# Gathering expert rows in a mixture-of-experts stage: one float32 copy and one pair of experts at a time, in place of two rounded copies and two pairs

## Chip, cores and metric

The kernel runs on one core of a Trainium2 chip, as one program. The metric is the device time of one execution in microseconds. It is compared with the same program with the change applied; the inputs, the outputs and the arithmetic asked for are the same.

## What is computed

The program is a whole block of a model: a first layer with two mixers and a mixture of experts, then two layers of another kind. The change touches the mixture of experts of the first layer alone. There are 256 tokens of width 1024, 32 experts in 4 groups, and each token goes to its two best experts of its best group. Cut to that part, the reference is:

```python
def hier_moe(h, w_rg, b_rg, w_re, b_re, w_eg, w_eu, w_ed):
    t = h.reshape(-1, d)                       # 256 x 1024, rmsnorm(x, norm2_g)
    lg = (t @ w_rg) + b_rg                     # 4 groups
    _, g_idx = lax.top_k(lg, 1)
    le = einsum('nd,dge->nge', t, w_re) + b_re # 8 experts in each group
    ...
    gates = sum(one_hot(eid) * (pg_sel * pw))  # 256 x 32, two entries in a row
    for e in range(32):
        hid = silu(t @ w_eg[e]) * (t @ w_eu[e])     # 1024 -> 512
        out = out + gates[:, e:e + 1] * (hid @ w_ed[e])  # 512 -> 1024
    return out
```

All of it is float32, and the three weights of an expert are 2 MB each, 192 MB for the 32 experts.

## The kernel before

**Tokens and places.** The tokens lie on the 128 partitions in two halves, `t` = 0 and 1. Each expert has 64 places for the tokens that come to it. `route` (from line 826 on) finds for each token its two experts and, by a product with a triangular matrix, its place in each; the result is `R`. `select` compares `R` with the numbers 1 to 64 and so makes a matrix of zeros and ones, tokens by places. A product of the normed tokens with that matrix, over both halves, gathers an expert's tokens; it comes out turned, width on the partitions and places on the columns, as `XT`.

**The pieces of h2.** `moe_rows` squares and turns each new half row of x (ScalarE and TensorE), and with the second half calls `rstd`, `route`, `select` and `moe_split`. The last makes two tiles of the rounded type float32r: `h2h`, the normed x rounded (ScalarE, L818), and `h2l`, what the rounding left (VectorE, L819). In `gather` (`add`, L960) both are multiplied with the selection of four experts (256 columns), each for both halves of the tokens: 8 pieces of the width x 2 x 2 = 32 products of 128 x 128 by 256. `turned` (L974, L976) scales by the norm's weight and copies the result out of PSUM, half of it on VectorE and half on ScalarE.

**The loop** takes 16 pairs of experts, i = 0 to 15. `front` multiplies the gathered tokens with the pair's `w_eg` and then `w_eu` (L1071); the two experts stand on the two halves of the array's columns, so each product has 64 columns of stationary operand. `hidden` computes silu(a) times b. `down` multiplies with `w_ed` one iteration later (L1098), and `scatter` brings the result back to the tokens one more iteration later (L1045, L1046, and the adds L1049). `middle` turns the hidden layer and the selection (L1017, L1025) and picks the gates (L1085). The order of TensorE's work is written out by hand: the calls named in the small tables given to `front` and `down` are put between their products. In every odd iteration but the last, four banks of the gather for the next two pairs are put among the products, two in the second `front` and two in `down`.

**Loads.** Each weight of an expert comes in two halves of 1 MB, on SyncE's queue, in the order of `expert_order`. They go round 18 slots: 8 of `wq`, 4 of `wp`, 6 of `wr` (`nwr`, L1947). `experts` takes four halves for one `front` or `down`, and four more are issued behind it (`expert_halves`). In the last round, from load 162 on, `wp` is left to the next layer's loads.

**The start of the stage.** For each half `t` of the tokens: add to x (L728), squares and transposes (L800, L803, L804), eight products with the router's weights (L834), a chain of small operations on VectorE up to the assignment `Asg` (L838 to L859), the places (L863 to L865), the selection (L824). For t = 1, `keep_warm` (L133) puts two products with zeros behind the router's. The first gather has its own order: t = 0 early, t = 1 when it can. `route_rest` counts the tokens of the fullest expert, and every engine branches on that count before the loop begins (L1108, L1109).

Of the kernel before, what the change touches and what calls it, by code (L numbers as in the profile page):

```python
# [19 lines left out]
P = 128  # L20
# [72 lines left out]
class K:  # L93
# [687 lines left out]
    def moe_open(self, es, e0):  # L781
# [14 lines left out]
    def moe_rows(self, x, t, n):  # L796
# [3 lines left out]
        nc.scalar.activation(self.h2l[:, t, cs], x[:, t, cs], AF.Square, accum_out=self.ss2[:, t, n:n + 1])  # L800
# [3 lines left out]
        nc.scalar.copy(self.hT32[:, 4 * n:4 * n + 4, t * P:(t + 1) * P], ps)  # L804
        if n == 1:
            r = self.rstd(self.ss2[:, t, 0:1], 1, D, 0, self.m1, self.ss2[:, t, 1:2])
            self.route(t, r)
            self.select(self.sel0, t, self.rt["R"], 0)
            self.moe_split(x, t, r)

    def moe_split(self, x, t, r):

        nc = self.nc
        for n in range(2):
            part = lambda z: z[:, t, n * 512:(n + 1) * 512].rearrange("p (k d) -> p d k", k=4)
# [11 lines left out]
    def route(self, t, r):  # L827
# [10 lines left out]
        v.scalar_tensor_tensor(T["L"], ps[:, 0:36], r[:, 0:1], self.br, op0=ALU.mult, op1=ALU.add)  # L838
# [99 lines left out]
    def moe(self, x, es, e0):  # L938
        nc, tc, A = self.nc, self.tc, self.A
        wg, wu, wd = A["w_eg"][0], A["w_eu"][0], A["w_ed"][0]  # L940
        p, h2h, h2l = self.m1, self.h2h, self.h2l
# [8 lines left out]
        def select(R_, e0, ne, pool, name):  # L950
            sel = pool.tile([P, NT, ne, 64], F32R, name=name, bufs=1)
# [3 lines left out]

        def gather(sel, n, XT=None):


            def add(ps, k, j, t, hp, start, stop, **kw):
                return nc.tensor.matmul(ps[:, j, :n], hp[:, t, (k + j) * P:(k + j + 1) * P],  # L960
                                        sel[:, t].rearrange("p e s -> p (e s)"), start=start, stop=stop, **kw)

            def bank(k):

                ps = self.mx.tile([P, 2, 256], F32, name="mx")
                for j in range(2):
                    for i, (hp, t) in enumerate(((h2h, 0), (h2h, 1), (h2l, 0), (h2l, 1))):
                        add(ps, k, j, t, hp, i == 0, i == 3)
                return ps

            def turned(k, ps, XT):
                if k % 4:
                    for j in range(2):
                        nc.scalar.activation(XT[:, k + j, :n], ps[:, j, :n], AF.Copy, scale=self.g2[:, k + j:k + j + 1])  # L974
                else:
                    nc.vector.tensor_tensor(XT[:, k:k + 2, :n], ps[:, :, :n],  # L976
                                            self.g2[:, k:k + 2].unsqueeze(2).to_broadcast([P, 2, n]), op=ALU.mult)

            if XT is None:
                return bank, turned  # L980

            banks = self.accT() + self.accT()
            with tc.high_priority(offset=3000):
                for hp in (h2h, h2l):
                    for ps, k in zip(banks, range(0, 8, 2)):
                        for j in range(2):
                            ins = add(ps, k, j, 0, hp, hp is h2h and j == 0, False, skip_group_check=True)
                            if hp is h2h and j == 0:
                                head = ins
                            elif hp is h2h:  # L990
                                tc.add_manual_dep(ins.ins, head.ins.name, mybir.DependencyInfo(
                                    mybir.DependencyClass.NoSync, mybir.DependencyReason.DATA))
            for ps, k in zip(banks, range(0, 8, 2)):
                for j in range(2):
                    add(ps, k, j, 1, h2h, False, False, skip_group_check=True)
            for ps, k in zip(banks, range(0, 8, 2)):
                for j in range(2):
                    add(ps, k, j, 1, h2l, False, True, skip_group_check=True)
                turned(k, ps, XT)

# [20 lines left out]
        def places(selw, rows, f=""):  # L1021

            pt = self.tp.tile([P, 4, P], F32, name="tp")
            for t in range(NT):
                nc.tensor.transpose(pt[:rows, t, :], selw[:, t].bitcast(F32), self.ident)  # L1025
# [25 lines left out]
        def scatter_last(sT, py, gs, po):  # L1051

            X2 = q.tile([P, 4, 512], F32, name="x2", tag="XT", bufs=1)
            for n in range(2):
                yh, yl = parts(py, n, P, gs)
                for t in range(NT):
                    nc.tensor.matmul(po[t][n], sT[:, t], yh, start=False, stop=False)
                for t in range(NT):
                    self.mm_last = nc.tensor.matmul(po[t][n], sT[:, t], yl, start=False, stop=True)
                    x2 = X2[:, 2 * n + t]  # L1060
# [4 lines left out]
        def front(ps, XT, i, between={}):  # L1065

            o = 2 * (i % 2)
            ww = self.experts()
            for k in range(8):
                for z in range(2):  # L1070
                    nc.tensor.matmul(ps[64 * z:64 * z + 64], XT[:, k, 64 * (o + z):64 * (o + z + 1)], ww[z][k],  # L1071
# [984 lines left out]
```

## Time and profile before

| | |
|---|---|
| median of 3 runs | 1799.76 us (1799.75 to 1799.99) |
| the profiled execution | 1796.94 us |
| its span | 1795.2 us |
| TensorE busy | 1738.4 us (97%) |
| VectorE, ScalarE, GpSimd busy | 976.9, 741.5, 112.2 us |
| moved by DMA | 414.51 MB, 231 GB/s on average |
| expert loads (three weights) | 192 of 1024 KB |

Times are microseconds from the start of the span. The stage in question runs from about 150 to about 633 us, the loop of the experts from 178.5 us on. In the page's 40 slices (45 us each), DMA moves 419 or 420 GB/s in all slices from the sixth to the thirteenth, and TensorE is at 9 tenths or more in nearly all. A matmul's recorded duration has its way through the array in it, and neighbours overlap; what a stream of them costs is the distance between their starts.

### The profile page before, as it was taken

To read this page: it belongs to the slowest core of one execution; us is meant where nothing else is said; L and a number is where in the kernel's file an instruction comes from. 1 tells how busy PE (TensorE), PEld (TensorE's weight loads), DVE (VectorE), ACT (ScalarE), POOL (GpSimd) and SP (SyncE) were. 2 spreads that over 40 slices of the span, in tenths; PEclk is the share of its full clock that TensorE was granted. 3 is DMA by queue.
4 is the path that set the end of the run, shared out by engine and by line. 5 is a ranking of instruction groups with operands and counts; after the bars stand their busy time and mean duration, and the time that the engine had idled before them with its cause. 6 is when DMAs were issued, how large, how long until landed. Compare 5 with 4: busy or idle time off the path is not lost. (4 is left out here: it accounts for less than half of the span.)

```text
span 1795.2 us, 27162 instructions
## 1 busy us (share of the span) xinstructions
PE 1738.4 (97%) x10927; PEld 1327.7 (74%) x10927; DVE 976.9 (54%) x1864; ACT 741.5 (41%) x1260; POOL 112.2 (6%) x157
## 2 busy tenths in 40 slices
PE   7999999999999989999999999999999999999998
PEld 6877433343334368799979999987879988999997
DVE  7676132222222177665666665557766467676555
ACT  3454111111011145565555454444556465455443
POOL 4110000000000040000012000003000001100000
PEclk8989999999999999999999999999999999999999
DMA  8447999999999964247545755554325644455552
GB/s 262 153 185 308 379 420 419 419 420 419 419 420 419 407 196 142 65 126 224 165 144 156 234 188 188 188 189 154 111 80 170 195 143 152 145 184 188 188 188 83
DMA packets 153465, 414.51 MB, mean 231 GB/s; under 512 B 13347, under 2 KB 42868, under 8 KB 128632
## 3 DMA queue, kind: packets, MB, share of 16 engines
q1 hardware_dynamic: 152408, 410.49, 63.8%
q0 software_dynamic: 784, 2.18, 0.3%
q8 instruction: 87, 1.43, 0.3%
q14 instruction: 42, 0.34, 0.1%
q10 hardware_dynamic: 144, 0.07, 0.0%
HBM read 411.63 MB, written 2.12 MB: 230 GB/s over the span
## 5 line engine op out<-in xcount | busy, mean ns | idle before, releaser
L170 DVE TENSOR_TENSOR wlo<-raw,whi 128x1024 fp32r<-128x1024 f32 (+4 forms) x372 | 440.3, 1184 | 305.9 <-ACT whi L169 305.2
L169 ACT CAST whi<-raw 128x1024 fp32r<-128x1024 f32 (+4 forms) x384 | 385.6, 1005 | 385.5 <-PE acc L231 156.6
L231 PE MATMUL acc<-xTl,whi 128*128 128x256 f32 x992 | 286.1, 290 | 1.2 <-DVE xTl L385 1.2
L231 PE MATMUL acc<-xTh,whi 128*128 128x256 f32 x992 | 286.0, 290 | 0.0
L231 PE MATMUL acc<-xTh,wlo 128*128 128x256 f32 x992 | 279.7, 289 | 0.0
L1071 PE MATMUL acc<-raw,XT 128*64 128x512 f32 x1024 | 237.7, 602 | 2.5 <-DMA raw<-in_w_eg 1.3
L231 PEld LDWEIGHTS acc<-xTl,whi 128*128 128x128 f32 x992 | 192.9, 195 | 6.8 <-issue 5.0
L231 PEld LDWEIGHTS acc<-xTh,whi 128*128 128x128 f32 x992 | 192.8, 195 | 6.5 <-issue 5.9
L231 PEld LDWEIGHTS acc<-xTh,wlo 128*128 128x128 f32 x992 | 189.2, 194 | 5.3 <-issue 4.9
L1071 PEld LDWEIGHTS acc<-raw,XT 128*64 128x64 f32 x1024 | 69.9, 137 | 127.5 <-issue 120.9
L178 PE MATMUL acc<-wlo,xTh 128*128 128x512 f32 (+4 forms) x368 | 129.7, 353 | 0.0
L177 PE MATMUL acc<-whi,xTh 128*128 128x512 f32 (+4 forms) x368 | 129.4, 352 | 0.0
L179 PE MATMUL acc<-whi,xTl 128*128 128x512 f32 (+4 forms) x368 | 128.5, 349 | 0.0
L1098 PE MATMUL acc<-raw,hidT 128*64 128x512 f32 x512 | 118.3, 596 | 1.4 <-DMA raw<-in_w_ed 1.4
L177 PE MATMUL acc<-whi,ffh 128*128 128x512 f32 x256 | 100.9, 394 | 0.0
L178 PE MATMUL acc<-wlo,ffh 128*128 128x512 f32 x256 | 100.7, 393 | 0.0
L179 PE MATMUL acc<-whi,ffl 128*128 128x512 f32 x256 | 100.7, 393 | 0.0
L1098 PEld LDWEIGHTS acc<-raw,hidT 128*64 128x64 f32 x512 | 36.5, 137 | 68.7 <-issue 61.2
L1036 DVE SCALAR_TENSOR_TENSOR yl<-acc,gs,yh 128x512 fp32r<-128x512 f32 x32 | 24.0, 751 | 103.8 <-ACT yh L1035 103.8
L1035 ACT ACTIVATE yh<-acc,gs 128x512 fp32r<-128x512 f32 x32 | 22.0, 687 | 136.5 <-PE acc L1098 136.5
L178 PEld LDWEIGHTS acc<-wlo,xTh 128*128 128x128 f32 x368 | 69.6, 189 | 8.3 <-issue 2.1
L177 PEld LDWEIGHTS acc<-whi,xTh 128*128 128x128 f32 x368 | 69.7, 189 | 7.5 <-issue 1.2
(687 smaller groups left out, 3128.6 us busy)
## 6 DMA issues: line engine op xcount, KB each, us to landing
raw<-in_w_in SPq DMA_DIRECT2D x70, 1024.0 KB, 5.2
raw<-in_w_eg SPq DMA_DIRECT2D x64, 1024.0 KB, 19.9
raw<-in_w_eu SPq DMA_DIRECT2D x64, 1024.0 KB, 19.9
raw<-in_w_ed SPq DMA_DIRECT2D x64, 1024.0 KB, 19.9
raw<-in_w_ff SPq DMA_DIRECT2D x64, 1024.0 KB, 5.1
raw<-in_w_out SPq DMA_DIRECT2D x12, 1024.0 KB
raw<-in_w_branch SPq DMA_DIRECT2D x12, 1024.0 KB, 5.8
raw<-in_w_in SPq DMA_DIRECT2D x8, 792.0 KB
```

What stands on the lines that cost most here:

```text
L169: nc.scalar.copy(hi[:, :nk, :n], src)
L170: ins = (nc.gpsimd if pool else nc.vector).tensor_sub(lo[:, :nk, :n], src, hi[:, :nk, :n])
L177: mm(ps, ahi, bhi, start=start, stop=False)
L178: mm(ps, ahi, blo, start=False, stop=False)
L179: self.mm_ins = mm(ps, alo, bhi, start=False, stop=stop)
L231: ins = mm(ps[c // 2][:, c % 2, :], w[:, j, c * P:(c + 1) * P], x[:, kx + k + j, :], start=first and c % 2 == 0, stop=k + j == nk - 1 and ...
L1035: nc.scalar.activation(yh[:rows], py[n][:rows], AF.Copy, scale=gs)
L1036: nc.vector.scalar_tensor_tensor(yl[:rows], py[n][:rows], gs, yh[:rows].bitcast(F32), op0=ALU.mult, op1=ALU.subtract)
L1071: nc.tensor.matmul(ps[64 * z:64 * z + 64], XT[:, k, 64 * (o + z):64 * (o + z + 1)], ww[z][k], start=k == 0, stop=k == 7)
L1098: nc.tensor.matmul(py[n][64 * z:64 * z + 64], hT[:, k, 64 * z:64 * z + 64], ww[z][k][:, n * 512:(n + 1) * 512], start=k == 0, stop=k == 3)
```

## The change

`h2h` and `h2l` become one tile `h2` in float32, and the second product with `h2l` goes, and with it L819. The gather is made for one pair of experts (128 columns) in place of two pairs (256 columns), in every iteration from 0 to 14, as plain float32 products: 8 pieces x 2 halves = 16 products of 128 x 128 by 128, in two banks of four pieces. The first bank is put behind the sixth piece of the second `front`, the second one behind the second step of `down` (for i = 0, behind the second `front`). VectorE alone copies them out. The selections take three buffers of two experts, `XT` two buffers of 128 columns, and the last scatter's scratch is cut to fit those. `nwr` goes from 6 to 7, so the loads go round 19 slots; the last round, without `wp`, then begins at load 152 and has 15. The router's eight products are written as two times four, each with its half of the row, and `keep_warm` behind them goes.

```diff
-        self.h2h = p.tile([P, NT, D], F32R, name="h2h")
-        self.h2l = p.tile([P, NT, D], F32R, name="h2l")
+        self.h2 = p.tile([P, NT, D], F32, name="h2")
-        self.sel0 = p.tile([P, NT, 4, 64], F32R, name="sel", bufs=1)
+        self.sel0 = p.tile([P, NT, 2, 64], F32, name="sel", bufs=3)
...
         nc.scalar.copy(self.hT32[:, 4 * n:4 * n + 4, t * P:(t + 1) * P], ps)
+        if n == 0:
+            self.logits = self.mx.tile([P, 512], F32, name="mx")
+        for k in range(4 * n, 4 * n + 4):
+            nc.tensor.matmul(self.logits[:, 0:36], self.hT32[:, k, t * P:(t + 1) * P], self.wr[:, k, :],
+                             start=k == 0, stop=k == 7)
...
-            h, lo = part(self.h2h), part(self.h2l)
             nc.scalar.activation(h, xs, AF.Copy, scale=r[:, 0:1])
-            nc.vector.scalar_tensor_tensor(lo, xs, r[:, 0:1], h.bitcast(F32), op0=ALU.mult, op1=ALU.subtract)
...
-        ps = self.mx.tile([P, 512], F32, name="mx")
-        for k in range(8):
-            ins = nc.tensor.matmul(ps[:, 0:36], self.hT32[:, k, t * P:(t + 1) * P], self.wr[:, k, :],
-                                   start=k == 0, stop=k == 7)
-        if t:
-            self.keep_warm(self.tp, "tp", 2, ins)
...
+            def add(ps, k, t, start, **kw):
+                return nc.tensor.matmul(ps[:, k % 4, :n], h2[:, t, k * P:(k + 1) * P],
+                                        sel[:, t].rearrange("p e s -> p (e s)"), start=start, stop=t == 1, **kw)
             def bank(k):
-                ps = self.mx.tile([P, 2, 256], F32, name="mx")
-                for j in range(2):
-                    for i, (hp, t) in enumerate(((h2h, 0), (h2h, 1), (h2l, 0), (h2l, 1))):
-                        add(ps, k, j, t, hp, i == 0, i == 3)
+                ps = self.mx.tile([P, 4, P], F32, name="mx")
+                for j in range(k, k + 4):
+                    for t in range(NT):
+                        add(ps, j, t, t == 0)
                 return ps
             def turned(k, ps, XT):
-                if k % 4:
-                    for j in range(2):
-                        nc.scalar.activation(XT[:, k + j, :n], ps[:, j, :n], AF.Copy, scale=self.g2[:, k + j:k + j + 1])
-                else:
-                    nc.vector.tensor_tensor(XT[:, k:k + 2, :n], ps[:, :, :n], ...
+                nc.vector.tensor_tensor(XT[:, k:k + 4, :n], ps[:, :, :n], ...
...
-            group, banks = i % 2 and i < 15, {}
-            if group:
-                sels[i // 2 + 1] = sel = select(R, 2 * i + 2, 4, p if i % 4 == 3 else q, "sel")
-                bank, turned = gather(sel, 256)
-            front(pu, XT, i, {0: (lambda: spread(1)) if i > 1 else lambda: None,
-                              5: lambda: take(0), 6: lambda: take(2)})
+            if i < 15:
+                sels[i + 1] = sel = select(R, 2 * i + 2, 2, p, name="sel", bufs=3)
+                bank, turned = gather(sel)
+                XT1, banks = q.tile([P, 8, P], F32, name="XT"), {}
+                take = lambda k: banks.update({k: bank(k)})
+                put = lambda k: turned(k, banks[k], XT1)
+            front(pu, XT, i, {0: (lambda: spread(1)) if i > 1 else lambda: None, 5: lambda: take(0)})
+            put(0)
             hid[i] = hidden(pg, pu, P)
...
             if i:
-                ys[i - 1] = down(mid[i - 1][0], {1: lambda: put(4), 3: lambda: put(6)})
+                ys[i - 1] = down(mid[i - 1][0], {1: lambda: take(4)})
+            else:
+                take(4)
+            put(4)
...
-        k.cnt, k.nwr, k.ready, k.order = 0, 6, deque(), k.expert_order()
+        k.cnt, k.nwr, k.ready, k.order = 0, 7, deque(), k.expert_order()
```

## Rows read from the trace of the kernel before

**Rows 1.** Busy time by stretch: us; PE, PEld, DVE, ACT, POOL; clock; DMA share; GB/s

```profile
178.50:500.00 321.50, 315.82 (x1512) 127.43 (x1513) 80.37 (x149) 44.86 (x85) 0.00 (x0) 1.00 1.00 413
500.00:620.00 120.00, 114.44 (x529) 47.25 (x528) 28.18 (x48) 15.97 (x30) 0.00 (x0) 0.99 1.01 419
```

**Rows 2.** The same view, each row one iteration of the loop: i = 2, 3, 11

```profile
220.11:245.33 25.22, 24.71 (x116) 9.13 (x114) 8.75 (x29) 4.46 (x8) 0.00 (x0) 1.00 1.01 419
245.33:275.69 30.36, 29.85 (x148) 12.78 (x146) 7.34 (x12) 5.80 (x10) 0.00 (x0) 1.00 1.01 420
...
467.60:498.00 30.40, 29.89 (x150) 12.81 (x148) 7.35 (x12) 4.51 (x9) 0.00 (x0) 1.00 1.01 420
```

**Rows 3.** Timeline of PE (start, us, engine, line, tiles, count), one bank's gather

```profile
262.42 0.40 PE L960 MATMUL mx<-sel,h2l 128*128 128x256 f32 x2
...
262.89 0.40 PE L960 MATMUL mx<-sel,h2l 128*128 128x256 f32 x2
263.21 1.08 PE L1071 MATMUL acc<-raw,XT 128*64 128x512 f32 x4
```

**Rows 4.** Timeline of PE, plain float32 products of 128 columns in an earlier stage

```profile
135.78 0.39 PE L673 MATMUL mx<-vd,aT 128*128 128x128 f32 x2
...
136.67 0.39 PE L673 MATMUL mx<-vd,aT 128*128 128x128 f32 x2
```

**Rows 5.** Timeline of PE, transposes of float32 among the experts' products

```profile
442.39 1.89 PE L1071 MATMUL acc<-raw,XT 128*64 128x512 f32 x8
444.21 0.66 PE L1017 MATMUL tp<-const,hid 128*128 128x128 f32 x4
444.70 0.38 PE L1025 MATMUL tp<-const,sel 128*128 128x128 f32 x2
```

**Rows 6.** Timeline of PE where it waited for loads, iterations 13 and 15

```profile
526.84 1.93 PE L1071 MATMUL acc<-raw,XT 128*64 128x512 f32 x6 [1.33 <-DMA raw<-in_w_eg]
528.70 0.66 PE L1017 MATMUL tp<-const,hid 128*128 128x128 f32 x4
...
606.95 4.46 PE L1098 MATMUL acc<-raw,hidT 128*64 128x512 f32 x18
...
615.33 0.66 PE L1017 MATMUL tp<-const,hid 128*128 128x128 f32 x4
```

**Rows 7.** Timeline of SyncE's queue, the expert loads as they are issued

```profile
564.26 7.80 SPq L930 DMA_DIRECT2D raw<-in_w_eg  x4
574.23 7.80 SPq L930 DMA_DIRECT2D raw<-in_w_eu  x4
```

**Rows 8.** Timeline of PE and DVE, from the router's last products to the loop

```profile
164.47 2.47 PE L834 MATMUL mx<-wr,hT 128*128 128x36 f32 x16
...
166.98 0.26 DVE L838 SCALAR_TENSOR_TENSOR L<-mx,rs_i,br 128x36 f32<-128x36 f32 x1 [0.88 <-PE mx L834]
...
167.79 1.09 DVE L819 SCALAR_TENSOR_TENSOR h2l<-x,rs_i,h2h 128x512 fp32r<-128x512 f32 x1
...
171.94 0.25 DVE L859 SCALAR_TENSOR_TENSOR Asg<-const,i,o 128x32 f32<-128x32 f32 x1
...
172.48 1.09 PE L133 MATMUL tp<-idle 128*64 128x512 f32 x2
173.51 0.41 PE L863 MATMUL mx<-Asg,const 128*128 128x32 f32 x2
...
178.55 15.67 PE L1071 MATMUL acc<-raw,XT 128*64 128x512 f32 x72 [1.15 <-DVEq L1109]
```

**Rows 9.** Busy time by stretch: the clock at the start; DMA as the loop begins

```profile
168.00:170.00 2.00, 2.00 (x6) 1.23 (x6) 2.00 (x4) 0.25 (x1) 0.00 (x0) 0.50 1.01 422
...
174.00:185.00 11.00, 9.14 (x52) 5.06 (x53) 3.66 (x16) 1.57 (x4) 0.00 (x0) 1.00 0.21 60
```

**Rows 10.** The gather's copies out of PSUM: duration in ns, minimum, median, maximum

```profile
L976 DVE TENSOR_TENSOR XT<-mx,g x14: 669/688/692, 211.8 to 550.8; 128x512 f32<-128x512 f32 x14
L974 ACT ACTIVATE XT<-mx,g x28: 466/472/476, 210.9 to 554.2; 128x256 f32<-128x256 f32 x28
```

More of the change, by code (lines that the diff above doesn't have):

```diff
@@ L831, in route @@
         T = {k: z[:, t] for k, z in self.rt.items()}
[L832 to L838 removed]
+        v.scalar_tensor_tensor(T["L"], self.logits[:, 0:36], r[:, 0:1], self.br, op0=ALU.mult, op1=ALU.add)
         iom = self.c("iota32m")
@@ L954, in select, with gather @@
             return sel
[L956 to L961, printed above, removed]
+        def gather(sel, first=False):
+            n = 64 * sel.shape[2]
+            def add(ps, k, t, start, **kw):
+                return nc.tensor.matmul(ps[:, k % 4, :n], h2[:, t, k * P:(k + 1) * P],
+                                        sel[:, t].rearrange("p e s -> p (e s)"), start=start, stop=t == 1, **kw)
@@ L980, in gather @@
+            if not first:
                 return bank, turned
-            banks = self.accT() + self.accT()
+            XT = q.tile([P, 8, P], F32, name="XT")
+            banks = [a.rearrange("p (a b) -> p a b", a=4) for a in self.accs(2, 1)]
             with tc.high_priority(offset=3000):
[L984 to L998, printed above, removed]
+                for k in range(8):
+                    ins = add(banks[k // 4], k, 0, k % 4 == 0, skip_group_check=True)
+                    if k % 4 == 0:
+                        head = ins
+                    else:
+                        tc.add_manual_dep(ins.ins, head.ins.name, mybir.DependencyInfo(
+                            mybir.DependencyClass.NoSync, mybir.DependencyReason.DATA))
@@ L999, in gather @@
+            for ps, k in zip(banks, (0, 4)):
+                for j in range(k, k + 4):
+                    add(ps, j, 1, False, skip_group_check=True)
                 turned(k, ps, XT)
+            return XT
         def hidden(pg, pu, rows, f=""):
@@ L1024, in places @@
             for t in range(NT):
-                nc.tensor.transpose(pt[:rows, t, :], selw[:, t].bitcast(F32), self.ident)
+                nc.tensor.transpose(pt[:rows, t, :], selw[:, t], self.ident)
             kw = dict(tag="s2", bufs=NS2) if f else dict(bufs=2)
@@ L1065, in front @@
         def front(ps, XT, i, between={}):
-            o = 2 * (i % 2)
             ww = self.experts()
@@ L1084, in middle @@
             for t in range(NT):
-                nc.tensor.matmul(pgs[:, 0:2], selw[:, t].bitcast(F32), G[:, t, 2 * i:2 * i + 2],
+                nc.tensor.matmul(pgs[:, 0:2], selw[:, t], G[:, t, 2 * i:2 * i + 2],
                                  start=t == 0, stop=t == 1)
@@ L1116, in more_rounds @@
                     nc.vector.tensor_copy(Gc, G[:, :, one])
-                    sel = select(Rc, 0, 1, q, "f_sel")
-                    XT = q.tile([P, 8, 64], F32, name="f_XT", tag="sel", bufs=1)
-                    bank, turned = gather(sel, 64)
-                    for k in range(0, 8, 2):
+                    sel = select(Rc, 0, 1, q, name="f_sel", bufs=1)
+                    XT = q.tile([P, 8, 64], F32, name="f_XT", tag="XT")
+                    bank, turned = gather(sel)
+                    for k in (0, 4):
                         turned(k, bank(k), XT)
@@ L1130, in more_rounds @@
                     for t in range(NT):
-                        nc.tensor.matmul(pgs[0:64, 0:1], sel[:, t, 0].bitcast(F32), Gc[:, t],
+                        nc.tensor.matmul(pgs[0:64, 0:1], sel[:, t, 0], Gc[:, t],
                                          start=t == 0, stop=t == 1)
@@ L1163, in moe @@
         sels[0] = self.sel0
-        XT = q.tile([P, 8, S], F32, name="XT", bufs=1)
-        gather(sels[0], 256, XT)
+        XT = gather(sels[0], True)
         G, mxi = self.route_rest(p)
@@ L1178, in moe @@
                               4: (lambda: spread(0)) if i > 1 else lambda: None})
-            group, banks = i % 2 and i < 15, {}
-            if group:
-                sels[i // 2 + 1] = sel = select(R, 2 * i + 2, 4, p if i % 4 == 3 else q, "sel")
-                bank, turned = gather(sel, 256)
-            take = lambda k: banks.update({k: bank(k)}) if group else None
-            put = lambda k: turned(k, banks[k] if k in banks else bank(k), XT) if group else None
-            front(pu, XT, i, {0: (lambda: spread(1)) if i > 1 else lambda: None,
-                              5: lambda: take(0), 6: lambda: take(2)})
+            take = put = lambda k: None
+            if i < 15:
+                sels[i + 1] = sel = select(R, 2 * i + 2, 2, p, name="sel", bufs=3)
+                bank, turned = gather(sel)
+                XT1, banks = q.tile([P, 8, P], F32, name="XT"), {}
[3 more added lines that the diff above has]
+            put(0)
             hid[i] = hidden(pg, pu, P)
-            if group:
-                XT = q.tile([P, 8, S], F32, name="XT", bufs=1)
-                put(0), put(2)
+            XT = XT1
             if i == 2 and "positions_2" in A:
```

29 lines of the change are left out of this document (14 added, 15 removed).

## Prediction

> **What bounds the kernel now.** I read busy time by stretch first. In the loop of the experts two resources are full at once [rows 1]: DMA has a share of 1.00 and 1.01 at 413 to 419 GB/s, and TensorE (PE) is busy 315.8 of 321.5 us and then 114.4 of 120.0. A busy share alone doesn't say which of them sets the time, so I read the timeline next, for two things: how far apart PE's products start, and what PE waits for.
>
> The experts' products are two instructions each, and the eight instructions of one row (four products) start over 444.21 - 442.39 = 1.82 us, 0.2275 us apart [rows 5]. An instruction that streams a row of 512 columns at 2.4 GHz needs 0.213, and the granted clock is 1.00 there. So PE streams without holes; the busy time isn't padding. Then the waits. An iteration without a gather takes 25.22 us and one with a gather 30.36 [rows 2]; the mean is 27.8. The loads come four in 574.23 - 564.26 = 9.97 us [rows 7], twelve in 29.9. PE is thus the faster one by 2.1 us an iteration and eats up the lead that the 18 full slots gave it. It catches up late: iteration 12 begins at 498.0 [rows 2], so the transposes of iteration 13 were due at 498.0 + 25.2 + 1.8 = 525.0 and came at 528.70 [rows 6], 3.7 us late, with waits for w_ed and w_eg before them. In iteration 15 thirty-two instructions of `down` from 606.95 on were due to end at 606.95 + 32 x 0.2275 = 614.2, and the next step came at 615.33 [rows 6], 1.1 us late. That makes 4.8 us of waiting in some 450 us. **The loop is bound by PE's own work until iteration 12, and by PE and DMA together from there on.** What is added to PE's work is added to the time, less these 4.8 us; what is taken from the loads can give back no more than 4.8 us.
>
> **The change, part by part.** *The gather in the loop.* Removed: seven gathers, each 30.36 - 25.22 = 5.14 us of PE [rows 2], 36.0 in all. One is four banks, 1.285 us each; eight products start (262.89 - 262.42) / 4 = 0.1175 us apart [rows 3], 0.94 a bank, so 0.345 us a bank is the price of breaking into the stream of 64-column products. Added: fifteen gathers of 16 plain float32 products of 128 columns. The trace has the same shape in an earlier stage: from 135.78 to 136.67 four products go by, two instructions each, 0.2225 us a product [rows 4]. Hence 16 x 0.2225 = 3.56 us a gather. A pair gets 16 products as before (32 were for two pairs), each half as wide, but each costs 1.9 times the float32r product of twice its width. To this come two breaks a gather. No row shows one for plain float32 products; the ends are nothing (the transposes, also float32 and 128 wide, follow the experts' products on their grid [rows 5]) and 0.345 (the float32r banks). I take 0.15, nearer the transposes, which share the type. So 3.86 us a gather and 57.9 in all; ends 53.4 and 63.8. **Net +21.9 us, between +17.4 and +27.8.**
>
> Here a rule of the Trainium skill speaks against this reading. Perfetto Trace Analysis, section Identifying the Most-Contended Engine, says that matmul busy share is a poor measure of TensorE's headroom, and that model FLOP use and the busy share of the weight loads should be taken instead. Here the weight loads are busy 127.43 of 321.50 us, 40% [rows 1], and by that the added products would be free beside a full DMA; that is the first rival below. The trace doesn't agree: the distance of 0.2275 us leaves no room.
>
> *The copies out of PSUM.* VectorE makes 30 of 0.688 us in place of 14, ScalarE's 28 of 0.472 go [rows 10]. VectorE is busy 7.3 to 8.8 us of an iteration [rows 2], so 0.7 more finds room. The next `front` needs the second bank only at its fifth piece, 16 instructions or 3.6 us after it begins, and in all iterations but the first the rest of `down` (24 instructions, 5.5 us) lies before that. I cost this at nothing; without the cover it is one copy, 0.7 us an iteration (the second rival). The selections, twice as many of half the width, are hidden in the same way. The three selection buffers and the two of `XT` are each read for the last time an iteration or more before they are written.
>
> *The slot.* One more load of 2.5 us can go out before the loop frees the first slot. DMA does stand idle there: from 174 to 185 us its share is 0.21 [rows 9], 8.7 us. But a load that lands earlier helps only where PE waits for one, and with 21.9 us more of PE's work it waits nowhere: its iteration of 25.22 + 3.86 = 29.1 us is still below 29.9, but over 15 iterations it gains only 12 us on DMA, where before it gained 32 to 33 and just caught up. So the lead of the loads is left unused at the end by some 20 us. Value of the slot: nothing. Value of the added work: the waits of **4.8 us** go.
>
> *The start.* The path is the router's last products, VectorE's chain to `Asg`, the places, the selection, the second half of the first gather, the copies and the branch. Half of the router's 16 instructions (2.47 us [rows 8]) move ahead, but for the last row they lie before the add that the chain begins with, as long as they fill PE there; I count 0.8 us for them, which is also what the logits waited for PE (0.88 [rows 8]). The two operations L819, the first of 1.09 us [rows 8], lie within VectorE's chain from 166.98 to 171.94, and go: 2.2 us. The zeros of `keep_warm` at 172.48 stand ahead of the places' product, which starts at 173.51, 1.3 us after `Asg` is there [rows 8]: at most 1.3. That is up to 4.3, but PE's clock was 0.50 there [rows 9], and with `keep_warm` gone nothing but the gather itself brings it back; eight products at half clock cost 8 x 0.2225 = 1.8 us more. I take **-3.0 us**; ends -4.5 and nothing. If the clock is still at its lower level when the loop begins, a `front`'s first 16 instructions cost 3.6 us more.
>
> **Sum** against the profiled execution of 1796.94 us: +21.9 - 4.8 - 3.0 = +14.1, that is 1811.0. The median of the runs is 2.8 us above that execution, so I expect **1814 us**. Ends: +17.4 - 4.8 - 4.5 = +8.1, or 1808; +27.8 - 4.8 = +23.0, or 1823, and 1826 with a cold clock.
>
> **Rivals.** *DMA sets the end (the other side).* If PE had room after all, the loads alone would set the time. They would begin the closed loop one load earlier (2.5 us) and the first slot would be freed 3.0 us earlier, which the idle 8.7 us [rows 9] can take in: 1799.8 - 5.5 = 1794. For it: DMA's share of 1.01 and PE's waits at the end [rows 1, 6]. Against it: the grid of 0.2275 us [rows 5] and that the waits are only 4.8 us. It decides if a new gather costs less than (36.0 + 4.8 + 3.0) / 15 = 2.9 us, 0.18 us a product without any break; the only row for such a product shows 0.2225 [rows 4]. By the Trainium skill's rule on the weight loads this would be the case. Chance 0.10.
>
> *A new wait for VectorE.* All copies now lie on one engine with an order of its own, between `hidden`, the adds of `scatter` and the selections, and the banks are two. If PE waits for one copy in each iteration, 15 x 0.7 = 10 us come on top: 1824. For it: TensorE's order is fixed by hand, so one late copy holds all behind it. Against it: VectorE is busy under a third of the time [rows 2]. Chance 0.12.
>
> *Little difference.* No breaks, the whole gain at the start, and some of it again where the next layer opens, since its loads are queued behind the experts' and would land earlier: 1808 less some 5, about 1803. It also covers the case that the change doesn't do what it says, because the extra slot isn't what the loads wait for. Chance 0.06.
>
> **How the numbers follow.** My forecast (1806 to 1823) has a chance of 0.72. The predicted time is its 1814. The range of 1804 to 1827 takes in the bounds of the breaks, the start and the second rival, and leaves out the first and most of the third. A change under 0.2%, 3.6 us, is about what a measurement of this kernel can't tell from none. Faster than 1796.2: 0.10, the first rival. Within 0.2%: 0.06. Slower than 1803.4: 0.84.
>
> **What would show it.** Iterations should all take 29 us, odd and even alike, with 32 gather instructions of 128 columns, 0.11 us apart, in each of the first fifteen. PE's waits for `raw` at 520 to 528 and 611 us should be gone, and the loop should end some 14 us later. The loop should begin at about 175.5 in place of 178.5 us. I am wrong in the main step if the products start closer than 0.2 us a product or iterations take less than 28 us; wrong in the cover if PE waits for the copies in many iterations; and wrong about the start if the clock is 0.50 into the first `front`.

## The result, and the profile after

| | before | after |
|---|---|---|
| median of 4 runs each | 1799.76 us | 1818.34 us (1817.98 to 1826.74) |
| ratio, 95% interval | | 1.0117 (1.0087 to 1.0146) |
| the profiled execution | 1796.94 us | 1817.98 us |
| its span | 1795.2 us | 1816.2 us |
| last product of the mixer (L179) to first product of the loop | 17.61 us | 14.89 us |
| the loop, to the first product of the next stage (L306) | 454.11 us | 478.74 us |
| from there to the end of the span | 1162.54 us | 1161.90 us |

The changed kernel is 1.2% slower by the ratio, which goes by the means of the runs, and 1.0% by the medians; one run of four, 1826.74 us, makes the difference. The last three rows are distances between starts in the two traces. All that was lost was lost inside the loop, 24.6 us, and 2.7 us were won ahead of it. Behind the loop nothing changed.

First, busy time by stretch of after, with the columns of [rows 1]: the two stretches of [rows 1], two iterations as in [rows 2], and one place late in the loop.

```profile
178.50:500.00 321.50, 315.86 (x1598) 138.10 (x1596) 86.45 (x166) 33.27 (x58) 0.00 (x0) 1.00 1.01 416
500.00:620.00 120.00, 117.68 (x594) 53.96 (x592) 30.27 (x51) 12.87 (x23) 0.00 (x0) 0.97 0.96 389
250.04:279.53 29.49, 28.98 (x148) 12.67 (x146) 8.00 (x14) 4.11 (x6) 0.00 (x0) 1.00 1.01 419
279.53:309.03 29.50, 28.99 (x149) 12.67 (x147) 7.99 (x14) 2.83 (x5) 0.00 (x0) 1.00 1.01 419
576.00:582.00 6.00, 5.73 (x28) 4.08 (x28) 1.55 (x3) 1.90 (x4) 0.00 (x0) 0.61 1.01 421
```

Odd and even iterations now take the same 29.5 us, where it was 25.22 and 30.36 by turns [rows 2]. PE's busy time in the first stretch is the same as before to 0.04 us, though the loop is slower: the busy share was full already and can't show it. Nor does the number of instructions (1598 in place of 1512), since a gather's instructions are shorter than the experts'. What shows it is the length of the iterations and, late, DMA's share, which falls from 1.01 to 0.96. The rates of the page's 40 slices say the same: where before held 419 GB/s through slice 13, after falls to 403, 366 and 360 from slice 12 on.

```profile
GB/s 260 152 199 318 417 420 419 420 419 419 420 403 366 360 121 191 71 95 221 172 126 144 246 189 188 192 193 161 125 71 156 198 162 132 159 185 186 186 186 82
```

The loads have stopped being a limit. The list of PE's waits from 175 to 660 us has no load any more (engine, line; total us, times, longest), and the places of [rows 6] now run through. In the timeline of PE, the 32 instructions of `down` in the last iteration take 636.96 - 629.99 = 6.97 us, where they took 8.38 before.

```profile
PE tp L1074 <- ACT hidT L1009: 8.2, 16, 0.5
PE acc L1061 <- DVEq L1098: 1.3, 1, 1.3
PE tp L306 <- ACT raw L1145: 0.3, 1, 0.3
```

```profile
629.99 7.04 PE L1087 MATMUL acc<-raw,hidT 128*64 128x512 f32 x32
636.96 0.66 PE L1008 MATMUL tp<-const,hid 128*128 128x128 f32 x4
```

One iteration of after in the timeline of PE, from its first `front` to the next one. The two rows of L958 are the banks of its gather:

```profile
250.04 1.89 PE L1061 MATMUL acc<-raw,XT 128*64 128x512 f32 x8
...
266.79 2.05 PE L958 MATMUL mx<-sel,h 128*128 128x128 f32 x16
268.77 1.94 PE L1061 MATMUL acc<-raw,XT 128*64 128x512 f32 x8
270.53 1.89 PE L1087 MATMUL acc<-raw,hidT 128*64 128x512 f32 x8
272.35 2.05 PE L958 MATMUL mx<-sel,h 128*128 128x128 f32 x16
...
279.53 1.89 PE L1061 MATMUL acc<-raw,XT 128*64 128x512 f32 x8
```

The rest of an iteration is what it was, so a gather costs 29.49 - 25.22 = 4.27 us. Its 16 products at the 0.2225 us of [rows 4] are 3.56, and 0.71 are left: 0.355 us for each of the two places where the stream is broken. The sum of the loop then closes: 15 x 4.27 = 64.05 in place of 36.0 is +28.05; the waits of 4.8 us went; and one group of small products cost 1.3 us more, since PE's clock was lower there (the last row of the first table, 0.61; 16 instructions of L306 in 3.39 us against 2.05 of the same kind just before). 28.05 - 4.8 + 1.3 = 24.6, and 24.63 was measured. The 1.3 us belong to the execution and not to the change: the same group took 2.05 us in x5_joined_banks, whose gather is still the new one, and 3.37 and 3.59 in x3_start_only and x8_rest_behind, whose loop is that of before.

### The profile page after: what moved, and what is told of

Read it like the earlier page. It is cut to its first block, busy times and chain, and to the rows that moved or that the text cites. A ratio compares the mean times of both kernels' runs of the same rounds, so it can differ in the third digit from the quotient of the medians.

```text
span 1816.2 us, 27688 instructions
## 1 busy us (share of the span) xinstructions
PE 1762.0 (97%) x11179; PEld 1353.6 (75%) x11179; DVE 985.5 (54%) x1892; ACT 727.7 (40%) x1228; POOL 109.3 (6%) x157
## 5 line engine op out<-in xcount | busy, mean ns | idle before, releaser
L1061 PE MATMUL acc<-raw,XT 128*64 128x512 f32 x1024 | 237.1, 602 | 1.3 <-DVEq L1098 1.3
L1061 PEld LDWEIGHTS acc<-raw,XT 128*64 128x64 f32 x1024 | 68.4, 137 | 126.3 <-issue 122.2
L179 PE MATMUL acc<-whi,xTl 128*128 128x512 f32 (+4 forms) x368 | 129.3, 351 | 0.0
L179 PE MATMUL acc<-whi,ffl 128*128 128x512 f32 x256 | 100.5, 393 | 0.0
L970 DVE TENSOR_TENSOR XT<-mx,g 128x512 f32<-128x512 f32 x30 | 20.7, 691 | 119.9 <-PE mx L958 119.9
```

Of the source, the lines that this page charges most:

```text
L179: self.mm_ins = mm(ps, alo, bhi, start=False, stop=stop)
L970: nc.vector.tensor_tensor(XT[:, k:k + 4, :n], ps[:, :, :n], self.g2[:, k:k + 4].unsqueeze(2).to_broadcast([P, 4, n]), op=ALU.mult)
L1061: nc.tensor.matmul(ps[64 * z:64 * z + 64], XT[:, k, 64 * z:64 * z + 64], ww[z][k], start=k == 0, stop=k == 7)
```

## Experiments

Each kernel ran against the kernel before on the same chip; "start" is the distance from the mixer's last product to the loop, "loop" its length, both from the trace. The median of the kernel before was 1797.24 us beside x1 to x3, 1796.84 beside x4 to x7, and 1799.07 beside x8 and x9, so medians compare within these three groups. Distances from the mixer are used because the mixer itself ends at different times: its last product starts at 160.94 us in before and at 165.96 in x9_joined_before, whose edit lies in the loop alone.

| kernel | median us | ratio to before (95%) | start | loop |
|---|---|---|---|---|
| x1_six_slots | 1819.09 | 1.0118 (1.0100 to 1.0137) | 14.87 | 478.75 |
| x2_rounded | 1792.26 | 0.9972 (0.9962 to 0.9983) | 13.46 | 454.29 |
| x2b_rounded_six_slots | 1795.97 | 0.9993 (0.9983 to 1.0002) | 13.05 | 456.68 |
| x3_start_only | 1798.90 | 1.0008 (0.9996 to 1.0020) | 18.15 | 454.51 |
| x4_float32_four | 1816.71 | 1.0105 (1.0084 to 1.0125) | 16.39 | 472.86 |
| x5_joined_banks | 1813.80 | 1.0096 (1.0070 to 1.0122) | 14.82 | 471.99 |
| x6_rounded_four | 1792.86 | 0.9975 (0.9964 to 0.9986) | 13.34 | 454.04 |
| x7_later_rest | 1797.12 | 0.9999 (0.9988 to 1.0010) | 17.38 | 454.04 |
| x8_rest_behind | 1800.31 | 1.0009 (0.9998 to 1.0019) | 18.50 | 454.12 |
| x9_joined_before | 1798.05 | 0.9994 (0.9981 to 1.0006) | 16.11 | 454.08 |

The theory: in after, PE's own work sets the loop, the float32 gather is what was added to it, and before stood within a few us of what its loads allow. Its rivals: the loads (or the new slots' order) set the loop; VectorE's copies hold PE; the time lies in something else that the change does. In the trace of x9 the start has the program of before, so it shows what a start varies by: 16.11 us where before took 17.61.

### x1_six_slots: after with one slot less

```diff
-        k.cnt, k.nwr, k.ready, k.order = 0, 7, deque(), k.expert_order()
+        k.cnt, k.nwr, k.ready, k.order = 0, 6, deque(), k.expert_order()
```

> The changed kernel with 18 slots in place of 19 (nwr 6), all else as changed. Theory 1 (PE's own work sets the loop, the loads have some 20 us of unused lead): no difference to the changed kernel, 1818 us within 1.5, iterations of 29.49 us, no wait of PE for raw but perhaps in the last two iterations. Rival (the lead of the loads carries the loop): one load less of lead, 2.5 us or more slower, 1821 us or above.

The loop took 478.75 us, with the slot 478.74. Where PE sets the time, a slot for loads is worth nothing.

### x2_rounded and x2b_rounded_six_slots: after with the gather in float32r

```diff
-        self.h2 = p.tile([P, NT, D], F32, name="h2")
-        self.sel0 = p.tile([P, NT, 2, 64], F32, name="sel", bufs=3)
+        self.h2 = p.tile([P, NT, D], F32R, name="h2")
+        self.sel0 = p.tile([P, NT, 2, 64], F32R, name="sel", bufs=3)
...
```

The rest of the diff gives the loop's selections the same type and reads them back as float32 elsewhere. The second kernel has `nwr` at 6 besides.

> The changed kernel with h2 and the selection rounded to float32r: the same 16 products of 128 columns for a pair, at the same places; what the rounding leaves is left out of the gather. Theory 1: a product falls from 0.2225 us to about 0.1175, a gather from 4.27 to 2.6 us, the loop by 15 x 1.68 = 25 us; PE would then end at about 1793, where the loads begin to limit again (1794): 1793 to 1797 us, and PE waits for raw again late in the loop. Rival (narrow products and the second break in each iteration cost the time, whatever the type): 1815 us or above.

> The run with rounded h2, with 18 slots in place of 19; the low part is left out of the gather here too. Theory 1: where PE has room the loads end the loop, and a slot less puts them back by one load, 2.5 us: 1796 to 1799 us. Rival (a slot is worth nothing in any case): the same as with 19 slots, within 1 us.

Only the type of the gather's products differs from after, and the loop is back at 454.29 us. The timeline of PE of x2_rounded, one iteration:

```profile
249.73 1.89 PE L1061 MATMUL acc<-raw,XT 128*64 128x512 f32 x8
...
266.48 1.11 PE L958 MATMUL mx<-sel,h 128*128 128x128 f32 x8
267.52 1.94 PE L1061 MATMUL acc<-raw,XT 128*64 128x512 f32 x8
...
277.34 1.89 PE L1061 MATMUL acc<-raw,XT 128*64 128x512 f32 x8
```

277.34 - 249.73 = 27.61, so this gather costs 2.39 us, and fifteen of them 35.9, as much as the seven of before (36.0). Everything else of the change (the loop's new order, copies on VectorE alone, three selections) is in this kernel, and its iterations show no cost of it; the loop's whole length alone would not tell, since the loads come close to limiting it here too. With that the rival of the copies falls. The wait for loads that I expected isn't in the list of PE's waits; iteration 13 has 1.8 us more than the same instructions take in after (the first eight of `front` 2.88 us for 1.82, `down` 7.85 for 7.12), and what PE stood for there isn't named. Without the seventh slot the loop is 2.4 us longer and PE does wait for a load (timeline of PE of x2b_rounded_six_slots):

```profile
522.91 1.93 PE L1061 MATMUL acc<-raw,XT 128*64 128x512 f32 x6 [0.85 <-DMA raw<-in_w_eg]
```

So the slot has a value where PE has room for it: 2.4 us in the loop, 3.7 us between the medians. Yet x2b has the 18 slots of before and as much work on PE, and its loop is 456.68 - 454.11 = 2.57 us longer than that of before. Its iteration 0 accounts for that: 18.71 us where 13.75 (before) + 2.39 = 16.14 would be due, because PE's clock was lower in the first `front` (16 instructions in 6.08 us; 3.46 in before, at 1.00). The first slots come free that much later. x2_rounded and x6_rounded_four lost 2.0 and 2.1 us in the same place, so the slot itself is worth some 2 us by this estimate. Busy time by stretch of x2b over these instructions:

```profile
172.11:178.19 6.08, 6.08 (x16) 1.81 (x18) 0.00 (x0) 0.00 (x0) 0.00 (x0) 0.57 0.12 46
```

### x4_float32_four and x6_rounded_four: before with one copy of h2

Both keep the gather for four experts in seven iterations; the one is plain float32, the other float32r with a seventh slot.

```diff
-        self.h2l = p.tile([P, NT, D], F32R, name="h2l")
...
-                    for i, (hp, t) in enumerate(((h2h, 0), (h2h, 1), (h2l, 0), (h2l, 1))):
-                        add(ps, k, j, t, hp, i == 0, i == 3)
+                    for i, (hp, t) in enumerate(((h2h, 0), (h2h, 1))):
+                        add(ps, k, j, t, hp, i == 0, i == 1)
...
```

> The kernel before with one float32 copy of h2 (no L819) and plain float32 products of 256 columns, four experts at a time, four banks every second iteration, 18 slots, router and keep_warm as before. Theory 1 (the passes of plain float32 cost the time, not the narrow form): a product takes twice 0.2225 less its overhead, about 0.43 us, a gather 16 x 0.43 + 4 x 0.355 = 8.3 us for two pairs against 5.14; the loop lasts 449.3 + 7 x 3.2 = 471 us against 454.1 (before) and 478.7 (changed), and the stage before the loop is 2 to 3 us shorter than before: 14 us slower than before. Rival (pairs and narrow products cost it): a loop of 456 us or less, no slower than before.

> The kernel before with one copy of h2 rounded to float32r (what the rounding leaves is left out of the gather), four experts at a time, 19 slots. PE's own work in the loop falls to about 436 us. Theory 1 (the loads have a floor of their own: 456.7 us of loop with 18 slots, 454.2 with 19): the loop lasts 453 to 455 us all the same, PE waits for raw some 15 us, and the time is that of the run with rounded pairs, about 5 us below before. Rival (PE's work is what sets the loop there too): a loop of 437 to 442 us and a time 15 us or more below before.

x4_float32_four has nothing of the change but the single copy and its float32 products, and its loop is 18.75 us longer than that of before, three quarters of the whole loss. Two fronts of it, timeline of PE, around an iteration with a gather:

```profile
249.03 1.89 PE L1066 MATMUL acc<-raw,XT 128*64 128x512 f32 x8
...
282.56 1.89 PE L1066 MATMUL acc<-raw,XT 128*64 128x512 f32 x8
```

33.53 - 25.22 = 8.31 us a gather, 58.2 for seven; 58.2 - 36.0 - 4.8 + 1.1 (the clock at L306 again, 3.16 in place of 2.05 us) is 18.5. After pays one pair more in its loop, since its first gather fetches two experts and not four. The median lies 19.9 us above that of before, where I expected 14: the loop lost 18.75 us and not 17, the start gained 1.2 and not 2 to 3, and some 2 us lie outside these two and stay open. x6_rounded_four is the other side. Its gathers have half of before's products, 7 x 16 x 0.1175 = 13.2 us less of PE's work, and its loop is as long as that of before. The work comes back as waits for loads (list of PE's waits, two of its rows):

```profile
PE acc L1093 <- DMA raw<-in_w_ed: 4.2, 5, 1.3
PE acc L1066 <- DMA raw<-in_w_eg: 3.3, 4, 1.3
```

These are 7.5 us, half of what I expected. The iterations show more: 9 to 12 took 0.6, 3.7, 2.4 and 3.7 us longer than their like before them, 10.4 us, and iteration 0 lost the 2.1 us of the clock.

### x5_joined_banks and x9_joined_before: fewer breaks

In after, both banks of a gather go behind the same piece of the second `front` (first diff); in before, the four banks make two groups in place of four (second diff). The products are the same.

```diff
-            front(pu, XT, i, {0: (lambda: spread(1)) if i > 1 else lambda: None, 5: lambda: take(0)})
+            front(pu, XT, i, {0: (lambda: spread(1)) if i > 1 else lambda: None, 5: lambda: (take(0), take(4))})
...
-                ys[i - 1] = down(mid[i - 1][0], {1: lambda: take(4)})
-            else:
-                take(4)
+                ys[i - 1] = down(mid[i - 1][0], {})
```

```diff
-                              5: lambda: take(0), 6: lambda: take(2)})
+                              5: lambda: (take(0), take(2))})
...
-                ys[i - 1] = down(mid[i - 1][0], {1: lambda: put(4), 3: lambda: put(6)})
+                ys[i - 1] = down(mid[i - 1][0], {1: lambda: (put(4), put(6))})
```

> The changed kernel with the second bank of the gather right behind the first in the second front, in place of in down: the same products, one break less in each iteration. Theory 1 (a break into the experts' stream costs 0.35 us, not 0.15): iterations of 29.1 to 29.2 us in place of 29.49, the loop 4 to 5 us shorter than 478.7, the time 4 to 5 us below the changed kernel. Rival (VectorE's copies hold the two banks): PE waits for a bank in each iteration and the loop is as long as before this edit, or longer.

> The kernel before, with the four banks of a gather in two groups (two banks together in the second front, two together in down): 14 breaks less, 14 x 0.345 = 4.8 us less of PE's work, the same arithmetic. Theory 1 (the breaks cost what is read, and before is within 1 us of what its loads allow over the whole loop): an iteration with a gather falls from 30.36 to 29.65 while PE limits, PE's waits for loads at the end grow from 4.8 to 8 to 10 us, and the loop stays at 452 to 454: 1795 to 1797. Rival (PE's work bounds the whole loop): 449, 1792. If the breaks are not what they cost, iterations stay at 30.4.

The timeline of PE of x5_joined_banks, an iteration with its 32 instructions together:

```profile
249.26 1.89 PE L1061 MATMUL acc<-raw,XT 128*64 128x512 f32 x8
...
266.00 3.84 PE L958 MATMUL mx<-sel,h 128*128 128x128 f32 x32
269.77 1.94 PE L1061 MATMUL acc<-raw,XT 128*64 128x512 f32 x8
...
278.40 1.89 PE L1061 MATMUL acc<-raw,XT 128*64 128x512 f32 x8
```

278.40 - 249.26 = 29.14 us, 0.35 less than after for one break less. Fifteen of them are 5.3 us; the loop is 6.75 shorter, and 1.3 of the difference is the group of L306, which ran in 2.05 us here. The break is thus measured by itself. The same in x9_joined_before, its timeline of PE and two rows of its list of waits:

```profile
248.18 1.89 PE L1071 MATMUL acc<-raw,XT 128*64 128x512 f32 x8
...
277.85 1.89 PE L1071 MATMUL acc<-raw,XT 128*64 128x512 f32 x8
```

```profile
PE acc L1071 <- DMA raw<-in_w_eg: 2.7, 2, 1.3
PE acc L1098 <- DMA raw<-in_w_ed: 1.9, 2, 1.3
```

29.67 us in place of 30.36: 0.69 for two breaks. Yet the loop is 454.08 us, as long as ever; PE's waits for loads rose from 2.7 to 4.6 us in the list, and iterations 11 and 12 took 32.14 and 27.72 us, 5.0 more than their like before them (1.3 more in before). Before thus stood at the limit of its loads over the loop as a whole: what is taken from its PE is lost in waits, what is added beyond its waits is paid.

### x3_start_only, x7_later_rest, x8_rest_behind: the start

x3_start_only is before with the router in two parts and no `keep_warm`. x7_later_rest has L819 of t = 1 later in the program; x8_rest_behind ties it behind `Asg` on VectorE; the diff is that of x8, without the line that keeps `Asg`'s instruction for it.

```diff
-            nc.vector.scalar_tensor_tensor(lo, xs, r[:, 0:1], h.bitcast(F32), op0=ALU.mult, op1=ALU.subtract)
+            ins = nc.vector.scalar_tensor_tensor(lo, xs, r[:, 0:1], h.bitcast(F32), op0=ALU.mult, op1=ALU.subtract)
+            if t:
+                self.tc.add_manual_dep(ins.ins, self.asg_ins.ins.name, mybir.DependencyInfo(
+                    mybir.DependencyClass.NoSync, mybir.DependencyReason.DATA))
...
```

> The kernel before with only the router's products in two parts and without keep_warm (h2 in two rounded parts, four experts at a time, 18 slots). Theory 1: the loop begins 1 to 2 us earlier than at 178.5 us (the two operations L819 stay in VectorE's chain), the loads with it, and the time is 1798 us within 1. Rival (the zeros of keep_warm are what brings the clock back): the loop begins no earlier or runs its first products at the lower clock, 1800 us or above.

> The kernel before with only this moved: for the second half of the tokens, h2l (L819) is made behind route_rest in place of within the chain to Asg. Nothing is left out. Theory 1 (the two L819 within VectorE's chain are what the start gained, the router's order and keep_warm gave nothing): the loop begins 15.5 to 16.5 us after first_out's last product in place of 17.6, and the time is 1 to 2 us below before. Rival (the start's gain needs the router's two parts or the missing keep_warm): 17 us or more, no difference.

> The kernel before, with one order added on VectorE: for t = 1 the two operations of the rounding's rest (L819) may only come behind Asg. Theory 1 (they lie in VectorE's chain): from the logits (L838) to Asg it takes 3.2 us in place of 4.96. The rest then stands between Asg and R, so part of it comes back there, and the loop begins 0.5 to 1.8 us earlier after the last product of the mixer (gap 15.8 to 17.1 in place of 17.6). Rival (the shorter chain of the changed kernel had another cause, such as the router's products in two parts): L838 to Asg stays at 4.9 us. Either way the loop, which the loads hold at 454, gives most of it back: 1795 to 1797, no measurable difference.

None of the three starts got shorter by more than 0.23 us, against what I expected of each. The start of x9_joined_before, with no edit in it, came out 1.5 us shorter than that of before, so no difference of that size is an edit's by itself. To see where the time lies, the start is cut into four distances: from VectorE's add to x (L728, the last one) to the logits, from there to `Asg`, to `R`, and to the loop.

| kernel | add to logits | logits to `Asg` | `Asg` to `R` | `R` to loop |
|---|---|---|---|---|
| before | 4.88 | 4.96 | 2.46 | 4.15 |
| after | 3.71 | 3.16 | 0.99 | 6.06 |
| x3_start_only | 5.88 | 4.98 | 0.76 | 5.40 |
| x7_later_rest | 4.83 | 4.94 | 2.31 | 4.16 |
| x8_rest_behind | 5.86 | 3.17 | 3.36 | 4.95 |
| x4_float32_four | 6.44 | 3.17 | 0.75 | 5.11 |
| x9_joined_before | 4.60 | 4.97 | 1.21 | 4.17 |

The logits, `Asg`, `R` and the loop of after start in these rows of PE and VectorE (L834, L855, L861, L1061), with the second half of the first gather between, whose 16 instructions take 3.75 us, nearly twice as long as in the loop:

```profile
165.35 0.26 DVE L834 SCALAR_TENSOR_TENSOR L<-mx,rs_i,br 128x36 f32<-128x36 f32 x1 [0.30 <-PE mx L807]
168.51 0.25 DVE L855 SCALAR_TENSOR_TENSOR Asg<-const,i,o 128x32 f32<-128x32 f32 x1
169.50 0.19 DVE L861 SCALAR_TENSOR_TENSOR R<-mx,Asg 128x32 f32<-128x32 f32 x1 [0.40 <-PE mx L860]
170.46 3.75 PE L958 MATMUL acc<-sel,h 128*128 128x128 f32 x16 [0.57 <-DVE pw L879]
175.56 4.94 PE L1061 MATMUL acc<-raw,XT 128*64 128x512 f32 x22 [1.35 <-DVEq L1098]
```

Logits to `Asg` takes 4.94 to 4.98 us in the four kernels with L819 in that chain and 3.16 to 3.17 in the three without: L819 costs 1.8 us there. In x7_later_rest the edit didn't do what it was for. VectorE's order is made by the planner (the step that orders the instructions of an engine when the program is built; by hand is only TensorE's order in the loop), and the two operations (now L820) lie where they were:

```profile
167.93 0.25 DVE L844 SCALAR_TENSOR_TENSOR L<-mx,rs_i,br 128x36 f32<-128x36 f32 x1 [0.84 <-PE mx L840]
...
168.75 1.10 DVE L820 SCALAR_TENSOR_TENSOR h2l<-x,rs_i,h2h 128x512 fp32r<-128x512 f32 x1
...
169.88 1.10 DVE L820 SCALAR_TENSOR_TENSOR h2l<-x,rs_i,h2h 128x512 fp32r<-128x512 f32 x1
```

In x8_rest_behind they are behind `Asg`, and the time comes back at once: the second of them stands between `R` and the selection, for 1.08 us.

```profile
172.76 0.26 DVE L841 SCALAR_TENSOR_TENSOR L<-mx,rs_i,br 128x36 f32<-128x36 f32 x1 [1.86 <-PE mx L837]
175.93 0.25 DVE L862 SCALAR_TENSOR_TENSOR Asg<-const,i,o 128x32 f32<-128x32 f32 x1
...
179.29 0.19 DVE L868 SCALAR_TENSOR_TENSOR R<-mx,Asg 128x32 f32<-128x32 f32 x1 [2.04 <-PE mx L867]
179.40 1.08 DVE L819 SCALAR_TENSOR_TENSOR h2l<-x,rs_i,h2h 128x512 fp32r<-128x512 f32 x1
```

In x3_start_only the split router didn't move either: its 16 instructions are one group on PE, in 3.48 us where before took 2.47 [rows 8].

```profile
163.29 3.48 PE L808 MATMUL mx<-wr,hT 128*128 128x36 f32 x16
```

That lower speed isn't the edit's doing: x8_rest_behind, which leaves all of it as before, took 3.45 us for the same 16. Without `keep_warm`, `R` to the loop rose by 1.25 us: the second half of the first gather took 3.55 us at a granted clock of 0.54, in before 2.11 at 1.00. In all six kernels without `keep_warm` that clock was 0.50 to 0.54, in the six with it 0.89 to 1.00. `Asg` to `R` fell by 1.7 us as well, but that isn't shown to be `keep_warm`'s: it is 0.75 also in x4_float32_four, which keeps it (PE does its zeros there before `Asg` comes), and 1.21 in x9_joined_before, where nothing was edited:

```profile
176.69 0.25 DVE L859 SCALAR_TENSOR_TENSOR Asg<-const,i,o 128x32 f32<-128x32 f32 x1
...
177.90 0.19 DVE L865 SCALAR_TENSOR_TENSOR R<-mx,Asg 128x32 f32<-128x32 f32 x1 [0.62 <-PE mx L864]
```

So what `keep_warm` costs and gives back in all stays open. So does how much of the 1.2 us at the router in after is the split and how much the clock of that execution: add to logits takes 4.60 us in x9 and 4.88 in before without any edit, and x8, with none ahead of it, took 5.86. And in x6_rounded_four, whose program has the router whole, the planner put its 16 instructions on PE as two groups of eight all the same; add to logits took 3.94 us there.

## Why the prediction was right, and where its sum was off

- **What bounds the loop.** Right, and it decided the sign. Added work on PE was paid in full (24.6 us of 28.05 + 1.3 - 4.8), a slot was worth nothing (x1_six_slots), and the rival that the loads set the end is excluded: PE waits for no load in after. By the rule of the Trainium skill that stood against it (Perfetto Trace Analysis, section Identifying the Most-Contended Engine), the weight loads leave room: they are busy 138.10 of 321.50 us in after, 43%. The measurement decides against that rule here; model FLOP use, its other measure, was not worked out.
- **The gather.** The step that failed is the break. I read the products right (0.2225 us) and put 0.15 us on a break, "nearer the transposes, which share the type". It is 0.355, just above my upper end of 0.345, so a gather costs 4.27 in place of 3.86 us, 6.2 us over fifteen. The reading behind it was wrong. I took 0.2275 us [rows 5] as the grid of the experts' products and saw the transposes on it. The grid is 0.215 us an instruction, as the weight loads of after show by the pair (below; engine PEld), and 0.2178 over the 32 of `down` above with the switch at their end. It is a mean: two instructions start within 0.007 us of each other and the next two 0.42 later, so my comparison with the 0.213 us of one instruction's 512 columns fits by the mean alone. In the eight of [rows 5] a switch of 0.10 us was already contained, 8 x 0.215 + 0.10 = 1.82. So the transposes had shown the price of a switch, and I had spread it over the products. The two types break alike: 0.345 and 0.355.

```profile
179.04 0.14 PEld L1061 LDWEIGHTS acc<-raw,XT 128*64 128x64 f32 x2 [0.29 <-issue]
179.47 0.14 PEld L1061 LDWEIGHTS acc<-raw,XT 128*64 128x64 f32 x2 [0.29 <-issue]
```

- **The waits of 4.8 us.** Gone, as said.
- **The clock inside the loop.** Not in my sum: +1.3 us at L306, by the execution. The lower clock that I feared in the first `front` did not come in after (16 instructions start over 3.48 us, 3.46 in before); in x2_rounded, x2b and x6 it cost 2.0 to 2.6 us.
- **The copies and the selections.** Nothing, as said. (VectorE isn't busy under a third of each iteration, as I wrote: 8.75 of 25.22 us is 35%.) The 30 copies are 691 ns each, and PE waits for none of them. That rival is excluded. The rows of line L970, with the durations in ns (minimum, median, maximum) and what VectorE itself waited for before it, which is PE:

```profile
L970 DVE TENSOR_TENSOR XT<-mx,g x30: 690/691/692, 189.8 to 606.5; 128x512 f32<-128x512 f32 x30
...
  PE mx L958: 119.9, 30
```

- **The slot.** Nothing here, as said, and for the reason given: DMA has time left (360 GB/s late in the loop).
- **The start.** Predicted -3.0 us, and the loop begins at 175.56 in place of 178.55. The parts are near the terms as well: -1.2 for the router (0.8), -1.8 for L819 (2.2), -1.5 from `Asg` to `R` (up to 1.3 for `keep_warm`), and +1.9 behind it, where the gather ran at the lower clock (1.8). Shown are L819 and the clock of the gather. The other two are no larger than what a start varies by without an edit, so that they agree is in part luck.
- **The sum.** +14.1 against the profiled execution was predicted, +21.0 came, and the loop ended 21.6 us later and not 14: 6.2 for the breaks and 1.3 for the clock, less 0.6 behind the loop. The median is only 4.3 us above the forecast of 1814, because I added the 2.8 us by which the median of before lies above its profiled execution, and for after that is 0.4. Two errors partly cancelled.

No kernel with all of the arithmetic is measurably faster than before. x2_rounded and x6_rounded_four are, by 0.28% and 0.25%, and both lack the rest that rounding leaves. The nearest to a repair is x5_joined_banks, still 1.0% slower.

## What to carry to other kernels

Price a few products that are put into a stream of another shape by the difference of two iterations, with and without them, and not by their own spacing: here 0.35 us a visit came on top, whatever their type, so fewer and longer visits are worth more than a better spread. Where two resources are both full, find out how many microseconds lie between them before counting a gain: before had under 5 us on PE, so 13 us less of work shortened the loop by nothing, and 28 us more cost 24.6. And where a planner orders an engine, moving a line in the program isn't moving it on the engine; look at the trace before judging the idea.

## What the chip showed that I had not expected

- Going from products with 64 columns of stationary operand to ones with 128 and back costs 0.10 us at a switch, at the transposes and the scatter as at the gather, and 0.35 us for a visit of the gather in all. In the timeline of PE of after, two scatter products stand 0.23 us apart, and the expert product behind them comes after 0.32:

```profile
618.67 0.40 PE L1036 MATMUL mx<-yh,selT 128*128 128x512 f32 x1
618.90 0.39 PE L1037 MATMUL mx<-yl,selT 128*128 128x512 f32 x1
619.22 3.65 PE L1061 MATMUL acc<-raw,XT 128*64 128x512 f32 x16
```

- Halving the moving columns of a float32r product from 256 to 128 saved a tenth of its time: 0.1175 us [rows 3] against (2.39 - 0.71) / 16 = 0.105 in x2_rounded. A plain float32 product took half as long: (8.31 - 4 x 0.355) / 16 = 0.431 us in x4_float32_four for 256, 0.2225 for 128. At 128 columns plain float32 is thus 2.1 times as dear as float32r, at 256 columns 3.7 times.
- The same 16 instructions at the start took 2.47 and 3.45 us in two executions with nothing changed ahead of them, by the clock that was granted: 0.76 in before and 0.53 in x8_rest_behind (busy time by stretch over these instructions, in this order). These are means of stretches in which it stood in part at 0.50 (1.2 GHz) and in part at 1.00 (2.4 GHz). PE had stood idle for 1.5 and 0.7 us just before in both, so no row here says why they differ. A microsecond there is no evidence for an edit.

```profile
164.47:166.94 2.47, 2.47 (x19) 2.40 (x19) 1.40 (x8) 0.81 (x1) 0.00 (x0) 0.76 0.97 378
```

```profile
169.27:172.72 3.45, 3.45 (x19) 3.38 (x19) 1.40 (x8) 1.79 (x2) 0.00 (x0) 0.53 0.99 382
```
